# Sharing projection half products over eight attention head pairs, and reordering the last visit's scaling

## The chip, the cores and the metric

The kernel runs on one core of a Trainium2 chip. The metric is the device time of one execution in microseconds (us), taken as the median of several runs. A program of one core has five engines that run side by side and wait for each other by semaphores: PE (matrix products), DVE and ACT (element-wise work), POOL (element-wise work and some transfers) and SP (issues most transfers).

## The reference

One layer with two parallel branches, a Mamba-2 scan and a causal attention with forget gates, merged and projected. Only the attention and the products around it matter here:

```python
proj = h @ w_in            # -> z_ssm, xBC, dt, q, k, v, f, z_att, g_ssm, g_att
for blk in range(seqlen // 128):
    s = q[blk] @ k[:q1].T * scale + fcum[q] - fcum[k]     # causal
    outs.append(softmax(s) @ v[:q1])
y_att  = o * silu(z_att)
merged = sigmoid(g_ssm) * (y_ssm @ w_branch_ssm) + sigmoid(g_att) * (y_att @ w_branch_att)
out    = x + rmsnorm(merged @ w_out)
```

Sequence 1024, model width 1024, 16 heads of 64, all in float32. Products of two float32 matrices are formed from high and low parts (`h`, `l`), so each 512-column product over one 128-row block takes three matmuls.

## The kernel before, in words

Every projection is a Strassen-like scheme with seven products for two units of 128 columns: a `Pair` has steps 1 to 7, each one product of prepared weights (`wop`) with one prepared operand (`x0` to `x6`, here named by the tiles: x0 is b11, x1 b21, x2 -b22, x3 t1, x4 -t2, x5 t3, x6 t4). A step has 12 matmuls and is cut into two *halves* of six. A `Stream` holds all steps in one fixed list and hands them out half by half (`stream.halves(n)`), so that PE has work while another phase waits. With each half go the preparations: weights for the step three places on (lines L351, L352), the results (L404, L412, L414 to L418), the operands of the next weight matrix (L265 loads, L277 to L281 splits into high and low), and gate products (L1062).

The attention phase runs over eight head pairs (two heads each, `hp` 0 to 7) with six *visits* `g` 0 to 5, in all 48 visits `m`. A visit belongs to two query blocks against one half of the keys. It issues in this order: the scores (`scores`: matmuls into tiles `s`, then on DVE the running minimum L1467 and on ACT the exponential L1471 with row sums), the weighted values of the visit before (`weighted`: tiles `av`), some halves of the stream ("ahead"), the transposes of the probabilities into tiles `pt` and their copies `p` (L1508 on DVE, L1510 on ACT), and some more halves ("behind"). `s` and `pt` share four PSUM banks.

After every second visit the row sums of a group of rows are complete. Such a group `n` (0, 1 or 2 of a head pair) goes through a chain: `scale` makes the factors 1/l (L1375, L1376 for group 2; L1379 to L1384 for the others) in the tile `ns`, PE turns them (tile `pt` or, at the very end, `tp`), ACT copies them to `st` (L1393) and sends them to DRAM (L1394), `take` reads them back spread over all partitions as `rb` (SP, L1400), and one visit later `out` multiplies the attention outputs by them (L1431, L1432; L1425 for group 2). For the last head pair `out(1)` also forms the differences that the next weight matrix needs (L1556, L1557) and splits them into x4, x5 and x2 at once; it issues no transfer. The tiles `st`, `rb`, the gate loads and the results named `th` share one ring of four buffers.

`room(m)` decides how many halves visit `m` gets: the halves that are left up to step 6 of the first pair of `w_branch_att` (`ends[4]`), times the visit's share of the weights that are left. That step needs an operand that only the last rows of the attention make. A scheduler then orders the instructions of each engine; those that are pinned keep their program order.

The loop over the visits, with the two places that the change touches, begins at line 1640:

```python
            for hd, which in end(m - 2):
                if hd.last and which:
                    hd.out(which)
            ...
            ahead, behind = room(m)
            stream.halves(ahead)
            for hd, which in end(m):
                hd.scale(which)
```

`end(m)` gives the head pair and group that visit `m` completes.

Of the kernel before, what the change touches and what calls it, by code (L numbers as in the profile page):

```python
# [19 lines left out]
NK = D // P  # L20
# [66 lines left out]
def hybrid_layer(ctx: ExitStack, tc, a, out):  # L87
# [1047 lines left out]
    with tc.tile_pool(name="pro", bufs=1, reuse_waits="tile", side="right") as pro, tc.tile_pool(  # L1135
# [37 lines left out]
        def turned(tiles, k):  # L1173
            pt = prop.tile([P, HALF], F32, tag="pt", bufs=2, name="pt")
            for j in range(4):
                turn(pt[:, j * P : (j + 1) * P], tiles[j][:, k * P : (k + 1) * P]) 
            return pt
# [117 lines left out]
    with tc.tile_pool(name="att", bufs=1, reuse_waits="tile", side="right") as ap, tc.tile_pool(  # L1295
# [26 lines left out]
        def load_q(hp, pair):  # L1322

            t = ap.tile([P, 2, 256], F32R, tag="q", bufs=2, name="q")
            for n, dram in enumerate((qh_dram, ql_dram)):
                nc.sync.dma_start(t[:, n, :].bitcast(F32), dram[hp, :, pair[1] * P : pair[1] * P + 256])
            q[hp, pair] = t

        def load_k(hp, h):

            t = k[hp, h] = ap.tile([P, 2, HALF], F32R, tag=f"k{h}", name="k")
            for n, dram in enumerate((kh_dram, kl_dram)):
                nc.sync.dma_start(t[:, n, :].bitcast(F32), dram[hp, :, half(h)])
            f = fb[hp, h] = ap.tile([P, 2, HALF], F32, tag=f"fb{h}", name="fb")
            nc.sync.dma_start(f, f_dram[2 * hp : 2 * hp + 2, half(h)].unsqueeze(0).to_broadcast([P, 2, HALF]))

        def load_v(hp, h):
            v[hp, h] = ap.tile([P, 4, P], F32, tag=f"v{h}", name="v")
            pin(nc.sync.dma_start(v[hp, h], v_dram[hp][:, 4 * h : 4 * h + 4, :]))
# [96 lines left out]
        heads = {}  # L1436

        def scores(hp, g, u):

            pair, h = GROUPS[g]  # L1440
            i = pair[u]
            w = min(HALF, (i + 1) * P - h * HALF)
            s = [pp.tile([P, HALF], F32, tag="s", bufs=4, name="s") for e in range(2)]
            t, keys = q[hp, pair], k[hp, h]
            isl = slice(i % 2 * P, i % 2 * P + P)
            ops = [(t[:, x, isl], keys[:, y, 0:w]) for x, y in ((0, 0), (0, 1), (1, 0))]
            diagonal = h == i // 4
            for m, (x, y) in enumerate(ops):
                for e in range(2):
                    mm(  # L1450
                        s[e][:, 0:w], x[rows[e]], y[rows[e]], start=(m == 0), stop=(m == 2 and not diagonal),
                        skip_group_check=True,
                    )
            if diagonal:
                for n, (x, y) in enumerate(corner):
                    for e in range(2):
                        mm(
                            s[e][:, w - P : w], x[rows[e]], y[rows[e]], start=False, stop=(n == 1),
                            skip_group_check=True,
                        )  # L1460
            hd = heads[hp]
            for e in range(2):
                o = ex[:, e, u, 0:w]
                nm = hd.at(hd.nm, i, h, e)
                with tc.high_priority():
                    pin(
                        nc.vector.tensor_tensor_reduce(  # L1467
                            o, s[e][:, 0:w], fb[hp, h][:, e, 0:w], 1.0, 3.0e38, ALU.add, ALU.min, nm
                        )
                    )  # L1470
                    pin(nc.scalar.activation(o, o, AF.Exp, scale=-1.0, bias=nm, accum_out=hd.at(hd.sm, i, h, e)))  # L1471
# [42 lines left out]
        def weighted(hp, g, b, first, p, start, stop):  # L1514
            pair, h = GROUPS[g]
            n = (7 - pair[0]) // 2 if pair[0] > 3 else 2
            hd = heads[hp]
            if n not in hd.av:
                hd.av[n] = pp.tile([P, HALF], F32, tag="av", bufs=1, name="av")
            c0 = 256 * h if n < 2 else pair[1] * P  # L1520
            for e in range(2):
                mm(
                    hd.av[n][rows[e], c0 + first * P : c0 + 256], v[hp, h][:, b % 4, rows[e]], p[:, e, first:, :],
                    start=start, stop=stop, skip_group_check=True,
                )

        state, deferred = {}, []

        def fetched(name, j):
            y = small("y")  # L1530
            nc.sync.dma_start(y, ops_a.block(name, j))
            return y

        def difference_tile():
            return ap.tile([P, HALF], F32, tag="x", bufs=1, name="x")
# [44 lines left out]
        def loads(m):  # L1580

            hp, g = divmod(m, 6)
            more = hp + 1 < NK
            if g == 0:
                if hp:
                    load_v(hp, 0)
                if not m:

                    for j in range(KH):
                        stream.line += ops_s.differences(j, difference_tile, small)  # L1590
            if g == 1:
                load_q(hp, (3, 2))
            if g == 2 and more:
                load_k(hp + 1, 1)
            if g == 3:
                load_q(hp, (1, 0))
                if more:
                    load_v(hp + 1, 1)
                if hp >= KH:
                    state["t"] = difference_tile()  # L1600
                    nc.sync.dma_start(state["t"], ops_a.block("t1", hp - KH))
            if g == 4 and more:
                load_q(hp + 1, (7, 6))
            if g == (5 if more else 4) and hp >= KH:
                state["y"] = fetched("b11", hp - KH)
            if g == 5 and more:
                load_k(hp + 1, 0)
                load_q(hp + 1, (5, 4))

        def end(m):  # L1610

            hp, g = divmod(m, 6)
            if 0 <= hp < NK and g % 2:
                yield heads[hp], g // 2
# [7 lines left out]
        for _ in range(14):  # L1622
            stream.half()

        weights = (1.1, 1.1, 1.1, 1.1, 0.75, 0.95, 1.05, 0.85)

        rooms = [1.15, 1.15, 0.8, 1.15, 1.1, 0.75]
        left = [sum(rooms) * sum(weights)]

        def room(m):  # L1630

            share = weights[min(m // 6, NK - 1)] * rooms[m % 6]
            to = stream.steps.index((ends[4], 6))
            n = round((2 * (to - stream.at) - (stream.run is not None)) * share / left[0])
            left[0] -= share
            behind = n // 2 if n > 3 else min(max(n - 1, 0), 1)
            return n - behind, behind

        made = []
        for m in range(6 * NK + 1):  # L1640

            if m < 6 * NK:
                hp, g = divmod(m, 6)
                if not g:
                    heads[hp] = Heads(hp)
                for u in range(2):
                    scores(hp, g, u)
            for one in made:
                weighted(*one)
            for hd, which in end(m - 1):  # L1650
                hd.free(which)
            if m == 6 * NK:
                stream.release()
                heads[NK - 1].out(2)
                break
            for hd, which in end(m - 2):
                if hd.last and which:
                    hd.out(which)
            for fn in deferred:
                fn()  # L1660
            deferred.clear()
            stream.release()
            for hd, which in end(m):
                hd.settle(which)
            ahead, behind = room(m)
            stream.halves(ahead)

            for hd, which in end(m):
                hd.scale(which)
                hd.load_gates(which)  # L1670
            loads(m)
            made = turned(hp, g, list(end(m - 1)))
            for hd, which in end(m - 2):
                if not hd.last or not which:
                    hd.out(which)
            if m == 6 * NK - 1:
                tp = pp.tile([P, HALF], F32, tag="s", bufs=4, name="tp")
                heads[hp].turn(2, tp)
                heads[hp].send(2, tp)
            stream.hold()  # L1680
            stream.halves(behind)
            for hd, which in end(m if m == 6 * NK - 1 else m - 1):
                hd.take(which)
# [59 lines left out]
```

## Time and profile before

| what | value |
|---|---|
| median of 3 runs | 1290.88 us (1290.15 to 1292.31) |
| the profiled execution, its own time | 1291.84 us |
| its span (first to last instruction) | 1290.1 us |
| granted TensorE clock over the span | 0.996 |
| attention phase in the trace | about 687 to 1133 us |

The page of the profile gives busy times by engine, the chain of work that ended last, and groups of instructions by line. The trace answers queries: the waits of an engine in a stretch, busy times and granted clock in stretches, and the instructions in order of time, each with the idle time before it and what ended it in square brackets. A half product of the stream shows as six matmuls of 128x512 with the operand's name (`x0h`, `x0l`).

### The profile page before, as it was taken

To read this page: it belongs to the slowest core of one execution; us is meant where nothing else is said; L and a number is where in the kernel's file an instruction comes from. 1 tells how busy PE (TensorE), PEld (TensorE's weight loads), DVE (VectorE), ACT (ScalarE), POOL (GpSimd) and SP (SyncE) were. 2 spreads that over 40 slices of the span, in tenths; PEclk is the share of its full clock that TensorE was granted. 3 is DMA by queue.
4 is the path that set the end of the run, shared out by engine and by line. 5 is a ranking of instruction groups with operands and counts; after the bars stand their busy time and mean duration, and the time that the engine had idled before them with its cause. 6 is when DMAs were issued, how large, how long until landed. Compare 5 with 4: busy or idle time off the path is not lost.

```text
span 1290.1 us, 20992 instructions
## 1 busy us (share of the span) xinstructions
PE 1255.2 (97%) x7054; PEld 987.4 (77%) x7054; DVE 1005.1 (78%) x1994; ACT 795.6 (62%) x1738; POOL 258.8 (20%) x250
## 2 busy tenths in 40 slices
PE   5999999999999999999999999999999999899997
PEld 3688888787888888888877777777777776678886
DVE  7988886987788978997767567666798767776975
ACT  7745665556665665566556666666786567644754
POOL 4000440013300330124101121110001102146052
PEclk9999999999999999999999999999999999999999
DMA  8232552646336533653365666667787568556932
GB/s 297 72 113 76 154 154 90 190 150 182 131 110 201 186 126 105 217 168 119 132 204 202 200 222 204 206 215 224 259 261 249 199 212 268 191 188 195 360 111 101
DMA packets 153515, 233.57 MB, mean 181 GB/s; under 512 B 15968, under 2 KB 61504, under 8 KB 153408
## 3 DMA queue, kind: packets, MB, share of 16 engines
q1 hardware_dynamic: 137408, 197.14, 48.0%
q10 hardware_dynamic: 11136, 19.11, 3.9%
q0 software_dynamic: 4864, 15.99, 3.2%
q8 instruction: 55, 0.90, 0.3%
q14 instruction: 52, 0.43, 0.1%
HBM read 162.99 MB, written 72.34 MB: 182 GB/s over the span
## 4 chain that ended last, share of the span: by engine, by line
PE 76%; DVE 8%; DMA 7%; ACT 4%; issue 2%; SPq 1%; ACTq 0%; DVEq 0%
PE pb L130 32%; PE pc L130 19%; PE pd L130 6%; PE s L130 5%; PE pt L133 5%; PE av L130 4%; PE yps L130 2%; DVE wop L352 2%; DMA raw<-in_wu 1%; DMA xt<-in_x 1%; PE st L130 1%; DVE sum L357 1%; DMA st_dram<-st 1%; PE tr L133 1%; PE tr_v L133 1%
## 5 line engine op out<-in xcount | busy, mean ns | idle before, releaser
L351 ACT ACTIVATE wop<-sum 128x512 fp32r<-128x512 f32 x180 | 112.5, 626 | 111.4 <-DVE sum L357 52.3
L352 DVE TENSOR_TENSOR wop<-sum,wop 128x512 fp32r<-128x512 f32 x180 | 137.1, 763 | 55.0 <-ACT wop L351 54.0
L1471 ACT ACTIVATE ex<-ex,nm 128x512 f32<-128x512 f32 (+1 forms) x192 | 116.3, 607 | 65.8 <-DVE nm L1467 62.5
L404 ACT ACTIVATE s<-pb 128x512 f32<-128x512 f32 x144 | 85.2, 591 | 99.7 <-PE pb L130 97.7
L130 PE MATMUL pc<-x3h,wop 128*128 128x512 f32 x384 | 130.6, 397 | 1.6 <-DVE th L414 1.3
L130 PE MATMUL pc<-x2h,wop 128*128 128x512 f32 x384 | 130.7, 398 | 0.6 <-DVE u L416 0.6
L130 PE MATMUL pb<-x0h,wop 128*128 128x512 f32 x384 | 131.0, 399 | 0.0
L130 PE MATMUL pb<-x5h,wop 128*128 128x512 f32 x384 | 129.8, 396 | 1.1 <-ACT s L404 1.1
L130 PE MATMUL pb<-x6h,wop 128*128 128x512 f32 x384 | 129.4, 395 | 1.3 <-ACT s L404 1.3
L352 DVE TENSOR_TENSOR wop<-raw,wop 128x512 fp32r<-128x512 f32 x144 | 101.0, 703 | 36.3 <-ACT wop L351 35.9
L130 PE MATMUL pb<-x4h,wop 128*128 128x512 f32 x384 | 129.2, 395 | 0.0
L1467 DVE CUSTOM_DVE_ANT_0 ex<-s,fb 128x512 f32<-128x512 f32 (+1 forms) x192 | 97.2, 552 | 20.0 <-PE s L130 19.9
L351 ACT ACTIVATE wop<-raw 128x512 fp32r<-128x512 f32 x144 | 89.7, 623 | 21.1 <-PE pc L130 13.6
L130 PE MATMUL pd<-x1h,wop 128*128 128x512 f32 x288 | 96.3, 394 | 0.0
L130 PEld LDWEIGHTS pc<-x3h,wop 128*128 128x128 f32 x384 | 72.3, 188 | 18.9 <-DVE th L414 1.7
L130 PEld LDWEIGHTS pb<-x5h,wop 128*128 128x128 f32 x384 | 72.1, 188 | 18.7 <-ACT s L404 2.2
L130 PEld LDWEIGHTS pc<-x2h,wop 128*128 128x128 f32 x384 | 72.1, 188 | 18.4 <-issue 2.8
L130 PEld LDWEIGHTS pb<-x6h,wop 128*128 128x128 f32 x384 | 72.1, 188 | 18.2 <-issue 1.9
L130 PEld LDWEIGHTS pb<-x0h,wop 128*128 128x128 f32 x384 | 72.7, 189 | 17.3 <-issue 2.7
L130 PEld LDWEIGHTS pb<-x4h,wop 128*128 128x128 f32 x384 | 72.3, 188 | 17.1 <-issue 2.3
L133 PE MATMUL pt<-ident,ex 128*128 128x128 f32 x576 | 75.4, 274 | 1.6 <-DVE nm L1467 0.6
L130 PE MATMUL s<-k,q 64*128 64x512 f32 (+3 forms) x576 | 73.6, 368 | 2.0 <-ACT p L1510 1.5
(310 smaller groups left out, 2915.8 us busy)
## 6 DMA issues: line engine op xcount, KB each, us to landing
raw<-in_wu SPq DMA_DIRECT2D x128, 256.0 KB
csb<-cs_dram SPq DMA_DIRECT2D x32, 256.0 KB
fb<-f_dram SPq DMA_DIRECT2D x16, 512.0 KB
rb<-st_dram SPq DMA_DIRECT2D x48, 128.0 KB
wd<-in_wo SPq DMA_DIRECT2D x40, 128.0 KB
xt<-in_x SPq DMA_DIRECT2D x8, 512.0 KB
gs_dram<-th ACTq DMA_DIRECT2D x16, 256.0 KB
qh_dram<-th ACTq DMA_DIRECT2D x16, 256.0 KB
```

What stands on the lines that cost most here:

```text
L130: return tc.keep_in_program_order(nc.tensor.matmul(*args, **kw))
L133: return tc.keep_in_program_order(nc.tensor.transpose(out_, in_, idn))
L351: nc.scalar.activation(op[:, 0], src, AF.Copy)
L352: nc.vector.tensor_tensor(op[:, 1], src, op[:, 0], ALU.subtract)
L357: self.adds.tensor_tensor(t, x, y, ALU.add)
L404: nc.scalar.activation(s, ps, AF.Copy)
L1467: nc.vector.tensor_tensor_reduce(o, s[e][:, 0:w], fb[hp, h][:, e, 0:w], 1.0, 3.0e38, ALU.add, ALU.min, nm)
L1471: pin(nc.scalar.activation(o, o, AF.Exp, scale=-1.0, bias=nm, accum_out=hd.at(hd.sm, i, h, e)))
```

## The change

It has two parts. The first is the table that shares out the halves. There are 156 of them from the start of the attention phase up to step 6 of `ends[4]` in both versions. Worked through `room`, the eight head pairs get 22, 22, 22, 22, 16, 16, 20 and 16 halves before, and 18, 18, 18, 19, 21, 19, 21 and 22 after. Inside a pair before, visits of the first four pairs have 4, 4, 3, 4, 4 and 3 halves, where 4 is two ahead and two behind and 3 is two ahead and one behind; in pairs 4, 5 and 7 it is 3, 3, 2, 3, 3 and 2, where 2 is one ahead and one behind. After, every visit of the first three pairs has 3, and no visit has 2. The last visit of all (pair 7, `g` 5) has one ahead and one behind before, and two ahead and two behind after.

The second part moves `out(1)` of the last head pair in that last visit from ahead of the halves to behind `scale(2)`, so that the last factors 1/l stand ahead of the products of the rows before them.

```diff
-        weights = (1.1, 1.1, 1.1, 1.1, 0.75, 0.95, 1.05, 0.85)
-        rooms = [1.15, 1.15, 0.8, 1.15, 1.1, 0.75]
-        left = [sum(rooms) * sum(weights)]
+        weights = (1.0, 1.0, 1.0, 1.0, 1.02, 1.02, 1.05, 1.15)
+        rooms = [1.1, 1.1, 0.85, 1.1, 1.05, 0.85]
+        left = [sum(rooms) * sum(weights) - weights[-1] * rooms[-1] + 1.4]

         def room(m):
-            share = weights[min(m // 6, NK - 1)] * rooms[m % 6]
+            share = weights[m // 6] * rooms[m % 6] if m < 6 * NK - 1 else 1.4
             to = stream.steps.index((ends[4], 6))
             n = round((2 * (to - stream.at) - (stream.run is not None)) * share / left[0])
             left[0] -= share
+            if m == 6 * NK - 1:
+                return n // 2, n - n // 2
             behind = n // 2 if n > 3 else min(max(n - 1, 0), 1)
             return n - behind, behind
...
             for hd, which in end(m - 2):
-                if hd.last and which:
+                if hd.last and which and m < 6 * NK - 1:
                     hd.out(which)
...
             for hd, which in end(m):
                 hd.scale(which)
                 hd.load_gates(which)
+            if m == 6 * NK - 1:
+                heads[hp].out(1)
+                for fn in deferred:
+                    fn()
+                deferred.clear()
```

The number of instructions on each engine stays the same. The places where the order differs most for what follows are in the last visit.

PE in the last visit, before: after the weighted values of visit 46 one half (x3, step 5 of `ends[4]`), six transposes of probabilities, and the turn of the last factors (`tp<-ident,ns`).

```order
L130 MATMUL av<-p,v 64x128 x2
L130 MATMUL pc<-x3h,wop 128x512
L130 MATMUL pc<-x3l,wop 128x512
L130 MATMUL pc<-x3h,wop 128x512 x2
L130 MATMUL pc<-x3l,wop 128x512
L130 MATMUL pc<-x3h,wop 128x512
L133 MATMUL pt<-ident,ex 128x128 x6
L133 MATMUL tp<-ident,ns 8x128
L130 MATMUL pc<-x3h,wop 128x512
```

The same place after: two halves (x6, step 4 of the last pair of `w_branch_ssm`) stand ahead of the transposes.

```order
L130 MATMUL av<-p,v 64x128 x2
L130 MATMUL pb<-x6h,wop 128x512
L130 MATMUL pb<-x6l,wop 128x512
L130 MATMUL pb<-x6h,wop 128x512 x2
L130 MATMUL pb<-x6l,wop 128x512
L130 MATMUL pb<-x6h,wop 128x512 x2
L130 MATMUL pb<-x6l,wop 128x512
L130 MATMUL pb<-x6h,wop 128x512 x2
L130 MATMUL pb<-x6l,wop 128x512
L130 MATMUL pb<-x6h,wop 128x512
L133 MATMUL pt<-ident,ex 128x128 x6
L133 MATMUL tp<-ident,ns 8x128
```

Step 5 with x3, which surrounded the turn before, now stands wholly behind it.

DVE in the last visit, before: after the last running minimum (`nm`) come the products of `out(1)` with `rb`, and the factors (L1375, L1376) between them.

```order
L1467 ISA nm 128x1
L1431 TENSOR_TENSOR o<-o,rb 128x512
L1432 TENSOR_TENSOR zr<-o 128x256
L1375 RECIPROCAL sm<-sm 128x8
L1556 TENSOR_TENSOR x<-zr,x 128x512
L1376 TENSOR_SCALAR ns<-sm 128x8
L1557 TENSOR_TENSOR y<-x,y 128x512
```

The same place after:

```order
L1467 ISA nm 128x1
L281 TENSOR_TENSOR x3l<-x3l,x3h 128x512
L1375 RECIPROCAL sm<-sm 128x8
L1376 TENSOR_SCALAR ns<-sm 128x8
L1431 TENSOR_TENSOR o<-o,rb 128x512
L281 TENSOR_TENSOR x3l<-x3l,x3h 128x512
L1432 TENSOR_TENSOR zr<-o 128x256
L281 TENSOR_TENSOR x3l<-x3l,x3h 128x512
L1556 TENSOR_TENSOR x<-zr,x 128x512
```

The factors are now ahead of L1431, and the low parts of two of the four blocks of x3 are behind it; by their addresses these are blocks 0 and 1, which step 5 takes first.

ACT in the last visit after, with the semaphores that each instruction waits for:

```order
L1471 ACTIVATE ex,sm<-ex,nm 128x128 [waits DVE_49] x2
L280 ACTIVATE x3h<-x3l 128x512 [waits DMAHW7_49]
L280 ACTIVATE x3h<-x3l 128x512 [waits DMAHW0_49]
L412 ACTIVATE th<-pb 128x512 [waits DMAHW5_49,DMAHW0_49,DMAHW7_49,DVE_49,PE_49]
L351 ACTIVATE wop<-raw 128x512 [waits DMAHW4_49]
L277 ACTIVATE x2h<-x2l 128x512 [waits DMAHW6_49]
L277 ACTIVATE x2h<-x2l 128x512 [waits DMAHW1_49]
L1510 ACTIVATE p<-pt 128x512 [waits PE_49]
L1510 ACTIVATE p<-pt 128x2x128 [waits Activation_49]
L1393 ACTIVATE st<-tp 8x128 [waits DMASW1_49,DMASW0_49,PE_49]
```

The result copy L412 takes over the buffer of `rb`, so its wait for DVE is a wait for L1431; the last two `p` copies and the copy of the turned factors `st` stand behind it. Before, L412 stood ahead of the last exponentials:

```order
L412 ACTIVATE th<-pb 128x512 [waits DMAHW1_49]
L1471 ACTIVATE ex,sm<-ex,nm 128x256 [waits DVE_49] x2
L1471 ACTIVATE ex,sm<-ex,nm 128x128 [waits DVE_49] x2
L1510 ACTIVATE p<-pt 128x512 [waits PE_49]
L1510 ACTIVATE p<-pt 128x2x128 [waits Activation_49]
L277 ACTIVATE x4h<-x 128x512 [waits DVE_49]
L1393 ACTIVATE st<-tp 8x128 [waits DMAHW6_49,DMASW0_49,PE_49]
```

There the `p` copies followed the exponentials directly. One visit earlier, in visit 46, the copy of group 1's factors (`st<-pt`, L1393) names a DVE semaphore among its waits before (by its value, L1062, the gate product whose buffer it takes); after, it names two transfers and PE alone.

## The prediction

> **What bounds the kernel now.** I read the page first, for which engine the end hangs on, from its busy times and its chain:
>
> ```profile
> PE 1255.2 (97%) x7054; PEld 987.4 (77%) x7054; DVE 1005.1 (78%) x1994; ACT 795.6 (62%) x1738; POOL 258.8 (20%) x250
> PE 76%; DVE 8%; DMA 7%; ACT 4%; issue 2%; SPq 1%; ACTq 0%; DVEq 0%
> ```
>
> PE is busy 97% of the span. The change leaves PE's matmuls as they are, so it can only win back time in which PE stands still or runs slowly, or add such time. Next I read the busy times by head pair (stretches between the last factors of successive pairs; the columns are the stretch and its length, then PE, PEld, DVE, ACT, POOL, granted clock, DMA share, GB/s):
>
> ```profile
> 738.80:798.00 59.20, 59.20 (x400) 45.25 (x399) 39.22 (x106) 36.79 (x92) 9.22 (x11) 1.00 0.65 208
> 915.00:965.00 50.00, 49.36 (x348) 36.74 (x347) 44.71 (x117) 41.91 (x104) 2.16 (x4) 1.00 0.83 274
> 965.00:1015.00 50.00, 50.00 (x364) 37.89 (x362) 39.52 (x110) 31.65 (x85) 4.86 (x9) 1.00 0.69 226
> 1068.80:1129.20 60.40, 54.40 (x359) 38.91 (x357) 46.04 (x115) 41.72 (x104) 11.08 (x14) 0.97 0.72 233
> ```
>
> Pair 1, with 22 halves, has no idle PE. Pair 5, with 16, has none either, so 16 halves were enough there. Pair 4 loses 0.64 us with DVE at 89%. Pair 7, with 16, loses 6.0 us (part of them before and after the pair's own visits) and its clock is below 1. So the time lies in the last pair. The waits of PE from 1090 to 1140 us, and for comparison from 870 to 980 us (total, count, longest):
>
> ```profile
> PE tp L133 <- DVE ns L1376: 3.3, 1, 3.3
> PE s L130 <- ACT p L1510: 1.2, 2, 1.1
> PE pb L130 <- ACT s L404: 0.7, 1, 0.7
> PE pt L133 <- ACT ex L1471: 0.6, 1, 0.6
> PE pt L133 <- DVE nm L1467: 0.3, 1, 0.3
> ```
>
> ```profile
> PE s L130 <- DVE p L1508: 0.4, 2, 0.2
> PE s L130 <- ACT p L1510: 0.3, 1, 0.3
> ```
>
> The longest wait is for the factors of the last group. The chain in order of time shows why they are late:
>
> ```profile
> 1117.93 0.10 ACT st L1393
> ...
> 1118.25 3.71 DMA st_dram<-st
> ...
> 1121.98 0.61 ACT th L412
> ...
> 1122.61 0.69 DVE th L1062
> ...
> 1123.84 3.46 DMA rb<-st_dram
> ...
> 1127.40 0.70 DVE o L1431
> ...
> 1129.20 0.18 DVE ns L1376
> ...
> 1129.42 0.27 PE tp L133
> ```
>
> The factors (L1376) stand on DVE behind L1431 of the preceding rows, and L1431 waits for `rb`, which has gone through DRAM and through the ring of four buffers (L412 and L1062 must free one first). The factors themselves need none of this.
>
> Each of the two longer waits is followed by a slow PE. The stretches:
>
> ```profile
> 1107.41:1118.52 11.11, 10.02 (x71) 7.60 (x70) 9.86 (x23) 8.16 (x21) 1.63 (x2) 1.00 0.41 127
> 1118.52:1123.84 5.32, 5.07 (x37) 3.22 (x37) 4.26 (x9) 3.69 (x8) 0.42 (x2) 0.68 0.63 193
> 1126.15:1129.42 3.27, 0.00 (x1) 0.00 (x1) 1.99 (x6) 0.98 (x3) 0.00 (x0) 1.00 0.07 23
> 1129.42:1132.97 3.55, 3.55 (x15) 1.97 (x15) 2.55 (x4) 2.92 (x6) 0.00 (x0) 0.64 0.01 5
> 1132.97:1139.90 6.93, 6.24 (x26) 4.87 (x25) 5.62 (x9) 3.20 (x6) 1.79 (x2) 0.94 0.85 267
> ```
>
> A clock of 0.68 over 5.32 us costs 5.32 x 0.32 = 1.70 us; 0.64 over 3.55 and 0.94 over 6.93 cost 1.28 + 0.42 = 1.70 us. So each fall costs 1.70 us.
>
> **The change, part by part.**
>
> *Factors ahead of `out(1)`.* Two short DVE instructions move ahead of L1431, L1432, L1556, L1557 and the splits of `out(1)`. The 3.27 us wait of the turn goes, since the factors then need only the last row sums, and the two halves ahead (one more than before) cover those. What is late next is `out(1)` itself, and what stands behind it: on DVE the low parts of x3 blocks 0 and 1, on ACT the result copy L412, the last two `p` copies and `st`. PE wants x3 first. These rows give PE's path from the turn of group 1's factors to it:
>
> ```profile
> 1089.74 0.62 PE L130 MATMUL s<-k,q 64*128 64x256 f32 x6
> 1092.76 0.50 PE L130 MATMUL pc<-x3h,wop 128*128 128x512 f32 x1
> 1100.25 0.50 PE L130 MATMUL pb<-x0h,wop 128*128 128x512 f32 x1
> 1103.10 0.78 PE L133 MATMUL pt<-ident,ex 128*128 128x128 f32 x3
> 1115.12 0.27 PE L133 MATMUL pt<-ident,ns 128*8 128x128 f32 x1
> 1115.80 0.48 PE L130 MATMUL pb<-x6h,wop 128*128 128x512 f32 x1
> 1118.52 1.09 PE L130 MATMUL s<-k,q 64*128 64x256 f32 x6 [1.09 <-ACT p L1510]
> 1125.33 0.82 PE L133 MATMUL pt<-ident,ex 128*128 128x128 f32 x6
> ```
>
> From the turn to the half behind 0.68; that half 1118.52 - 1.09 - 1115.80 = 1.63; scores and values of a visit of this shape 1092.76 - 1089.74 = 3.02; two halves 1103.10 - 1100.25 = 2.85; six transposes and a turn about 0.8. PE begins x3 about 9.0 us after the turn and needs its low part at 9.3. The other path is `st`, DRAM, `rb`, L1431 and one split. It took 1127.40 - 1117.93 = 9.47 us from `st` to L1431, of which 1123.84 - 1121.96 = 1.9 were the ring, leaving 7.6; a later trip took less:
>
> ```profile
> 1117.93 0.27 ACT L1393 ACTIVATE st<-pt 8x128 f32<-8x128 f32 x1 [0.69 <-PE pb L130]
> ...
> 1129.85 0.25 ACT L1393 ACTIVATE st<-tp 8x128 f32<-8x128 f32 x1
> ...
> 1135.17 0.69 DVE L1425 TENSOR_TENSOR zr<-o,rb 128x512 f32<-128x512 f32 x1 [0.19 <-DMA rb<-st_dram]
> ```
>
> The second trip is 1135.17 - 1129.85 = 5.3 us. With 1.3 for L1431 and a split, 6.6 to 8.9 us from `st`. `st` came 2.8 us after the turn. Of that 0.69 was idle, for the buffer that L1062 held, a wait it no longer has; the rest, 2.1, was other work of ACT, and the order now has one operation of some 0.5 less there (six after the exponentials instead of seven). So I let it start between 0.3 (at once) and 1.6 us after the turn. So x3 is ready 6.9 to 10.5 us after the turn, against 9.3: from 2.4 early to 1.2 late. I take 0.3, nearer to early since the ring's wait is gone. If `st` starts at 2.8 again, it is 11.7, 2.4 late, and with a fall of the clock 4.1. `out(1)` feeds x4 only one half pair later, and step 6 waits for nothing else of it.
>
> *Four halves in the last visit, three everywhere early.* The first four pairs lose halves behind the transposes: their visits with two behind fall to one. That cover serves the `p` copies, which free the banks for the next scores. Before, 29 visits had one behind, and together they show 0.7 + 1.25 us of such waits, 0.067 each. After, 36 have one, 7 more: 0.5 us; bounds 0 and 7 x 1.09 = 7.6. No visit has one half ahead any more (seven did), so the 0.61 us wait of transposes for exponentials goes. Of the 1.09 + 0.16 us in visit 47, most came from `st` 2.8 us late, since the `p` copies stand behind it on ACT: it goes with that wait.
>
> *More halves in pairs 4 to 7.* Pair 7 gets 22 instead of 16 and so the operand splits of x0 to x6 within fewer visits. Pair 4 shows what that costs where DVE is at 89%: 0.64 us in 50. I take 0.8 us for pair 7; bounds 0 and, for pairs 4 and 7 each, twice that, 3.2.
>
> *Sum.* Gone: 3.27 + 1.25 + 0.61 = 5.1 idle, and two falls of the clock, 3.4: 8.5 us. Come: 0.3 + 0.5 + 0.8 = 1.6. Net 6.9. The 0.69 us wait for L404 stays, and the rest of the program behind it is in the same PE order. Against the profiled execution's own 1291.84 us that is 1284.9. The median of the runs shown is 0.96 lower, at 1290.88, which would give 1284.0. I forecast midway: **1284.5 us**.
>
> [...] The second fall followed a wait of 3.27 us, the first one of 1.09 us. Elsewhere a wait as long left the clock alone:
>
> ```profile
> 675.66 0.50 PE L130 MATMUL pc<-x3h,wop 128*128 128x512 f32 x1 [1.28 <-DVE th L414]
> ```
>
> ```profile
> 675.66:679.00 3.34, 3.33 (x15) 2.76 (x16) 2.81 (x5) 1.71 (x4) 0.00 (x0) 1.00 1.05 402
> ```
>
> So 1.09 us of idleness alone does not make a fall; what stood around it differs (16 transposes and small score matmuls here, dense halves there). [...]
>
> **The rivals.**
>
> *The first fall stays* (transposes and small products cause it, not the gap): the gain is 1.70 us less, 1286.2. For it, the row at 675 us; against it, the many other visits of the same shape with a clock of 1.00 and no gap.
>
> *A new wait in the old one's place:* `st` is late again, L1431 holds x3 and the `p` copies, PE stands 2.4 us and the clock falls: 4.1 instead of 0.3, so 1288.3. For it, DVE and ACT both stand behind one trip through DRAM now; against it, the ring's waits are gone and PE has 1.4 us more to do first.
>
> *Slower: the early visits lose their cover.* In pairs 0 to 3, 15 visits go from two halves behind to one. If ACT (62% there) or DVE's own `p` copies are late, scores wait for banks. At the 1.09 us of visit 47 each it costs 15 x 1.09 = 16.4 us, 15.9 more than I took: 1300.4. It turns the result beyond 0.2% slower from (6.9 + 2.6) / 15 = 0.63 us a visit. Against it, pair 1's row: two of its six visits already have one half behind and PE is never idle; and pair 5 with one behind in all six.
>
> *No net change:* the waits move into pairs 4 to 7, where both DVE and transfers are densest (pair 4: DMA 0.83), and eat the gain: 1290.9.
>
> **How the numbers follow.** Forecast 0.55, first fall stays 0.15, new wait 0.12, early visits 0.10, no net change 0.08. A measurement of this kernel can tell about 0.2%, 2.6 us, from no change: faster means below 1288.3, slower above 1293.5. The first two and half of the third are faster, 0.76; the other half and nearly all of the last are the same, 0.13; the early visits and a rest of the last slower, 0.11. The range: below, everything gone and nothing come, 1290.88 - 8.5 = 1282.4; above, the new wait with the density term at its bound of 3.2 instead of 0.8, 1288.3 + 2.4 = 1290.7. That holds the first three, 0.82.
>
> **What would show it.** In the changed profile: no wait of `tp` for L1376; a clock of 1.00 from 1090 to 1140 us, or one fall (first rival); waits of scores for `p` below 2 us in all over the phase; `st` of visit 46 within 1.6 us of its turn; x3's first matmul behind `tp` without a wait above 1 us. The forecast is wrong if PE's idle time from 687 to 1137 us and the falls of the clock together do not come down from about 10 (the waits quoted, 6.8, and 3.4) to about 3 us.

## The result, and the profile after

After takes 1286.72 us (median of 10 runs, 1282.37 to 1289.42), before 1290.65 us beside it (10 runs, 1287.28 to 1294.19): a ratio of 0.9965, 95% interval 0.9953 to 0.9977. That is faster, inside the range, and 2.2 us above the forecast of 1284.5. Runs of one kernel differ by up to 10 us, so everything below goes by ratios, and a profile is one sample. The profiled execution of after took 1288.76 us.

First the page of after, its busy times:

```profile
PE 1253.9 (97%) x7054; PEld 987.4 (77%) x7054; DVE 1010.0 (78%) x1994; ACT 794.7 (62%) x1738; POOL 259.8 (20%) x250
```

PE is 1.3 us less busy than before and DVE 4.9 us more, which says nothing of where the time moved. The busy times by stretch do, from the first scores of the phase to the wait for L404 at its end, cut at 1090 us; before, then after:

```profile
686.77:1090.00 403.23, 402.10 (x2772) 305.41 (x2773) 288.77 (x780) 269.78 (x678) 51.41 (x70) 1.00 0.68 221
1090.00:1137.05 47.05, 40.64 (x253) 28.18 (x251) 37.45 (x86) 30.28 (x76) 8.01 (x10) 0.93 0.60 194
```

```profile
686.19:1090.00 403.81, 397.62 (x2735) 300.59 (x2735) 286.33 (x771) 264.84 (x668) 49.81 (x68) 0.99 0.65 216
1090.00:1134.61 44.61, 43.77 (x288) 32.55 (x287) 38.39 (x93) 34.60 (x86) 10.19 (x11) 1.00 0.69 234
```

Behind 1090 us PE's idle time goes from 6.41 to 0.84 us and the clock from 0.93 to 1.00 (47.05 x 0.07 = 3.3 us): some 8.9 us won. Ahead of 1090 us the idle time goes from 1.13 to 6.19 us and the clock to 0.99. So the last pair gained what was forecast, and most of it was given back earlier. PE's waits in after from 687 to 1145 us (total, count, longest):

```profile
PE pt L133 <- ACT ex L1471: 2.5, 2, 2.2
PE pt L133 <- DVE nm L1467: 2.5, 4, 1.5
PE s L130 <- ACT p L1510: 0.8, 2, 0.6
PE pb L130 <- ACT s L404: 0.7, 1, 0.7
PE s L130 <- DVE p L1508: 0.3, 1, 0.3
```

They add up to 6.8 us, as in before, but the two of the last pair (`tp` for L1376, scores for `p`) are gone but for 0.15 us, and two kinds that were 0.6 us each are 2.5 us each.

**The last visit of after**, from the timelines of PE, ACT and DVE:

```profile
1117.64 0.27 PE L133 MATMUL pt<-ident,ns 128*8 128x128 f32 x1
1119.21 0.25 ACT L1393 ACTIVATE st<-pt 8x128 f32<-8x128 f32 x1
...
1125.32 1.14 ACT L280 ACTIVATE x3h<-x3l 128x512 fp32r<-128x512 f32 x2
1126.57 0.60 ACT L412 ACTIVATE th<-pb 128x512 f32<-128x512 f32 x1
...
1125.68 0.17 DVE L1376 TENSOR_SCALAR ns<-sm 128x8 f32<-128x8 f32 x1
1125.76 0.69 DVE L1431 TENSOR_TENSOR o<-o,rb 128x512 f32<-128x512 f32 x1
...
1126.37 0.81 PE L133 MATMUL pt<-ident,ex 128*128 128x128 f32 x6
1127.03 0.27 PE L133 MATMUL tp<-ident,ns 128*8 128x128 f32 x1
1127.06 0.48 PE L130 MATMUL pc<-x3h,wop 128*128 128x512 f32 x1
```

The factors (L1376) come ahead of L1431, the turn `tp` stands directly behind the transposes, and x3 directly behind `tp`: no row has an idle time.

**Pair 5 of after.** The last factors (L1376) of pair 4 stand at 947.98 us, so what follows is the first visit of pair 5; the expectations further down call this place pair 4. Timeline of ACT, then of PE; then the busy times of the stretch in which the transposes wait and of the one behind it:

```profile
956.57 0.33 ACTq L622 DMA_DIRECT2D ga_dram<-th  x1
956.94 1.16 ACT L280 ACTIVATE x1h<-x1l 128x512 fp32r<-128x512 f32 x2 [4.47 <-DMA fb<-f_dram]
...
960.89 0.69 PE L133 MATMUL pt<-ident,ex 128*128 128x128 f32 x2 [2.25 <-ACT ex L1471]
962.19 1.81 PE L133 MATMUL pt<-ident,ex 128*128 128x128 f32 x6 [0.61 <-DVE nm L1467]
...
958.64:960.89 2.25, 0.01 (x2) 0.00 (x1) 2.25 (x7) 2.25 (x6) 0.54 (x1) 0.95 0.89 287
960.89:967.50 6.61, 6.00 (x21) 4.67 (x21) 5.92 (x13) 5.98 (x16) 1.08 (x2) 0.50 0.96 354
```

ACT stood for 4.47 us at the store of a gate (L622), which ACT issues itself. The store waited for the broadcast load into `fb`, which has nothing to do with its data; in the trace the two only count on the same DMA semaphore (number 102), one after the other. x1's splits, the maxima (L1467) and the exponentials (L1471) came that much later. PE stood 2.25 and 0.61 us. The clock fell at the end of the first wait (0.95 over it) and was 0.50 over the 6.61 us behind it, which is 3.3 us more, 0.3 of them while PE stood anyway.

**Pair 7 of after**, its second visit, DVE and PE:

```profile
1082.74 0.69 DVE L1062 SCALAR_TENSOR_TENSOR th<-th 128x512 f32<-128x512 f32 x1 [5.68 <-DMA th<-gs_dram]
...
1087.13 0.33 PE L133 MATMUL pt<-ident,ex 128*128 128x128 f32 x1 [1.46 <-DVE nm L1467]
```

The same kind of standing: DVE waits for a load of the gate, with the maxima queued behind L1062.

### The profile page after: what moved, and what is told of

Read it like the earlier page. It is cut to its first block, busy times and chain, and to the rows that moved or that the text cites. A ratio compares the mean times of both kernels' runs of the same rounds, so it can differ in the third digit from the quotient of the medians.

```text
span 1287.0 us, 20996 instructions
## 1 busy us (share of the span) xinstructions
PE 1253.9 (97%) x7054; PEld 987.4 (77%) x7054; DVE 1010.0 (78%) x1994; ACT 794.7 (62%) x1738; POOL 259.8 (20%) x250
## 4 chain that ended last, share of the span: by engine, by line
PE 73%; DVE 9%; DMA 8%; ACT 5%; issue 3%; SPq 1%; POOL 0%; ACTq 0%; DVEq 0%; POOLq 0%
PE pb L130 30%; PE pc L130 17%; PE pd L130 6%; PE av L130 5%; PE s L130 5%; PE pt L133 5%; PE yps L130 2%; DVE wop L352 2%; DMA raw<-in_wu 1%; DVE sum L357 1%; DMA xt<-in_x 1%; PE st L130 1%; DVE xs L771 1%; PE tr L133 1%; ACT wop L351 1%
## 5 line engine op out<-in xcount | busy, mean ns | idle before, releaser
L1471 ACT ACTIVATE ex<-ex,nm 128x512 f32<-128x512 f32 (+1 forms) x192 | 116.2, 606 | 71.8 <-DVE nm L1467 67.7
L404 ACT ACTIVATE s<-pb 128x512 f32<-128x512 f32 x144 | 85.1, 591 | 98.3 <-PE pb L130 95.3
L1467 DVE CUSTOM_DVE_ANT_0 ex<-s,fb 128x512 f32<-128x512 f32 (+1 forms) x192 | 96.9, 552 | 17.9 <-PE s L130 17.9
L133 PEld LDWEIGHTS pt<-ident,ex 128*128 128x128 f32 x576 | 67.4, 142 | 15.1 <-DVE nm L1467 4.3
```

The costliest lines, as they stand in the source:

```text
L133: return tc.keep_in_program_order(nc.tensor.transpose(out_, in_, idn))
L404: nc.scalar.activation(s, ps, AF.Copy)
L1467: nc.vector.tensor_tensor_reduce(o, s[e][:, 0:w], fb[hp, h][:, e, 0:w], 1.0, 3.0e38, ALU.add, ALU.min, nm)
```

## The experiments

The theory was that the gain is the last visit's and that the evenly shared table gives part of it back where engines that work in order stand behind late transfers. The rivals: order or halves alone make the gain; ACT and DVE are simply full at this place; what it shows is one run's accident.

### One half of the change at a time

Before with the order alone:

```
             for hd, which in end(m - 2):
-                if hd.last and which:
+                if hd.last and which and m < 6 * NK - 1:
                     hd.out(which)
...
+            if m == 6 * NK - 1:
+                heads[hp].out(1)
+                for fn in deferred:
+                    fn()
+                deferred.clear()
             loads(m)
```

> Before's table of halves (one ahead and one behind in the last visit), with only out(1) of the last pair moved behind the factors of the last group. Theory 1 (the gain lies in the last visit; order and halves each carry a part): the 3.27 us wait of the turn for the factors goes and with it the fall of the clock behind it, 1.7 us, but PE now has one half less on its way to x3, so x3 waits up to 2.9 us for its low part, and the 1.09 us wait with its fall further ahead may stay: 1286 to 1289 us where before has 1290.7. Theory 2 (the order alone does all of it): as after or below, 1283 to 1286.7. Theory 3 (only the halves count; without them the wait for the factors just turns into one for x3, as long and with the same fall): 1290 to 1291.

1287.79 us, ratio 0.9975 (0.9963 to 0.9987): inside the range of theory 1. The wait of `tp` is gone, but PE waits elsewhere in the last pair (timeline of PE), and behind the first of these waits the clock falls once (0.85 and 0.81 in the two stretches of 5 us from 1100 us):

```profile
1102.15 0.33 PE L133 MATMUL pt<-ident,ex 128*128 128x128 f32 x1 [0.88 <-DVE nm L1467]
...
1130.59 0.50 PE L130 MATMUL pb<-x4l,wop 128*128 128x512 f32 x1 [1.32 <-DVE x4l L278]
```

The x3 that it was to wait for came in time; x4 did not, with one half less in between. Theory 2 is not ruled out: 1287.79 lies above its range, but the interval holds after's 0.9965, and the quotients of the medians are 0.9968 here (before took 1291.86 us beside it) and 0.9970 for after.

After with the table alone (the diff above taken out of after):

> After's table of halves (four in the last visit), with out(1) at its old place ahead of the factors. Theory 1: two more halves give PE about 2.8 us more work there; the one ahead covers 1.4 of the 3.27 us wait, so some 1.9 us of it stay, with a fall of the clock or without: 1288.5 to 1290.5. Theory 2 (the order does all of it): the table brings nothing by itself, and its denser late pairs cost: 1291 to 1294. Theory 3 (only the halves count): as after, 1286.7.

1293.10 us, ratio 1.0019 (1.0006 to 1.0033). The time is the one of theory 2, but the reason is another than its denser pairs alone. PE, DVE and ACT in the last visit of that kernel:

```profile
1122.08 0.27 PE L133 MATMUL tp<-ident,ns 128*8 128x128 f32 x1
1126.80 0.50 PE L130 MATMUL pc<-x3h,wop 128*128 128x512 f32 x1 [4.45 <-ACT x3h L280]
...
1120.28 0.69 DVE L1431 TENSOR_TENSOR o<-o,rb 128x512 f32<-128x512 f32 x1
1121.34 0.16 DVE L1376 TENSOR_SCALAR ns<-sm 128x8 f32<-128x8 f32 x1
...
1126.13 1.13 ACT L280 ACTIVATE x3h<-x3l 128x512 fp32r<-128x512 f32 x2
```

`tp` does not wait here either, though L1431 still stands ahead of the factors: with more halves in the pair, `rb` lands in time. But `out(1)` now also puts its operand copies ahead of x3's on ACT (x3h at 1126.13; in after at 1125.32, ahead of L412), and PE stands 4.45 us for them. So the table needs the order: alone it costs 0.19%, both together win 0.35%, and these intervals are far apart. That the order needs the table is not shown: alone it wins 0.25%, which cannot be told from both.

### Is it the even table?

After with before's weights and rooms, the last visit kept at four:

```
-        weights = (1.0, 1.0, 1.0, 1.0, 1.02, 1.02, 1.05, 1.15)
+        weights = (1.1, 1.1, 1.1, 1.1, 0.75, 0.95, 1.05, 0.85)
-        rooms = [1.1, 1.1, 0.85, 1.1, 1.05, 0.85]
+        rooms = [1.15, 1.15, 0.8, 1.15, 1.1, 0.75]
```

> After's order and four halves in the last visit, with before's weights and rooms for all other visits: per pair 22, 22, 22, 21, 15, 16, 20, 18 halves where after has 18, 18, 18, 19, 21, 19, 21, 22. Theory 1 (the evenly shared table gives back some 4 us in pairs 4 to 7, where more halves put transfers and operand copies into fewer microseconds): no wait for exponentials and no fall of the clock in pair 4, 1281.5 to 1284. Rival (the table costs nothing; what after shows in pairs 4 and 7 varies from run to run and would come here as well): 1286.7 as after. Rival (one half ahead in visits 2 and 4 of pairs 4 and 7 leaves transposes waiting for exponentials): 1287 or more with waits on the exponentials of over 2 us in all.

1290.31 us, ratio 0.9992 (0.9979 to 1.0006): theory 1 missed. Without the even table the kernel is slower than after, and the intervals lie apart, if barely. The last rival has the time but not its waits. They are for ACT's `p`, 4.8 us in all, and the largest has the same cause as in after, at another place (chain in order of time, then PE and the stretch):

```profile
930.82 3.82 DMA rb<-st_dram
...
934.72 0.33 ACTq L622
...
935.09 1.09 ACT p L1510 x2
```

```profile
935.74 0.32 PE L130 MATMUL s<-k,q 64*128 64x128 f32 x1 [1.91 <-ACT p L1510]
...
935.00:940.00 5.00, 4.09 (x26) 2.64 (x26) 4.08 (x16) 4.24 (x13) 0.54 (x1) 0.66 0.97 317
```

A gate store holds ACT until an `rb` load has landed, 2.2 us. With either table a store meets a late load; the table decides which. Before's profile has one as well: behind a gate store at 953 us ACT stands 2.3 us for a load of `q`, and PE waits no more than 0.3 us there.

### The gate stores off ACT's queue

After with L622 on GpSimd's queue:

```
-            nc.scalar.dma_start(dram[i, :, half(ch)], t[ch])
+            pin(nc.gpsimd.dma_start(dram[i, :, half(ch)], t[ch]))
```

> After, with the stores of the tanh gates (L622) issued on GpSimd's queue instead of ScalarE's. In after's profile such a store held ScalarE 4.47 us in pair 4, until an unrelated broadcast load into fb had landed; exponentials came late, PE stood 2.25 and 0.61 us and its clock was 0.50 for 6.6 us. Theory 1 (this standing still is what the density of pair 4 costs): no such waits and no fall in pair 4, 2.9 + 3.3 = 6.2 us less if every run of after has it, 1.5 to 6 us less than after in the median, 1281 to 1285. Rival (ScalarE and VectorE are simply full in pair 4): the exponentials are as late without the store, 1286.7 as after. Rival (GpSimd's stores hold up its own additions or stores, which feed PE): 1287 to 1290.

1284.95 us, ratio 0.9953 (0.9936 to 0.9969), at the upper end of theory 1's range. Beside later kernels it was run once more:

> The kernel of e4_gate_store once more (after, with the gate stores on GpSimd's queue), because six runs gave 0.9953 with an interval that still touches after's 0.9965. Theory (ScalarE standing behind gate stores costs after 1 to 3 us): 0.993 to 0.9955, no wait for exponentials above 0.6 us in pair 4. Rival (no more than chance): 0.996 to 0.997.

1284.72 us, 0.9951 (0.9933 to 0.9968). And after itself once more:

> After itself once more, as a reference for the runs beside it and for a second profile of the same program. Theory (where PE stands is set by the program; the microseconds vary with when transfers land): waits on exponentials or their maxima in pair 4 and pair 7 again, the falls of the clock in other places or numbers, ratio to before 0.9965 +- 0.0015. Rival (pair 4's wait was one run's accident): no wait above 0.5 us in pair 4.

1286.83 us, 0.9965 (0.9951 to 0.9978). Each of the two intervals of the stores moved overlaps after's, but both runs lie on the same side of after by nearly the same. The repeated after has the waits of pair 5 again, behind the same store, and half the slow time (timeline of PE, then a stretch, then ACT's wait):

```profile
957.57 0.44 PE L133 MATMUL pt<-ident,ex 128*128 128x128 f32 x2 [1.38 <-ACT ex L1471]
958.87 1.25 PE L133 MATMUL pt<-ident,ex 128*128 128x128 f32 x6 [0.86 <-DVE nm L1467]
...
960.00:965.00 5.00, 5.00 (x25) 4.01 (x24) 4.38 (x8) 5.00 (x13) 1.08 (x2) 0.66 1.04 389
...
ACT x1h L280 <- DMA fb<-f_dram: 3.6, 1, 3.6
```

The run of the table alone shows the same wait of ACT, with 2.6 us. So it is no accident of one run.

Pairs 4 and 5 in one stretch, 900 to 1010 us, of before, after, after again, the stores moved, and the stores moved again, in this order:

```profile
900.00:1010.00 110.00, 109.36 (x767) 82.70 (x765) 89.68 (x234) 81.61 (x205) 7.02 (x13) 1.00 0.76 247
```

```profile
900.00:1010.00 110.00, 106.08 (x707) 79.62 (x706) 83.77 (x221) 78.15 (x193) 7.22 (x12) 0.97 0.71 237
```

```profile
900.00:1010.00 110.00, 106.85 (x716) 80.07 (x713) 85.13 (x224) 78.22 (x191) 7.36 (x13) 0.98 0.73 244
```

```profile
900.00:1010.00 110.00, 107.31 (x736) 80.14 (x735) 86.40 (x227) 77.64 (x191) 12.29 (x22) 1.00 0.74 251
```

```profile
900.00:1010.00 110.00, 106.73 (x722) 80.15 (x720) 84.94 (x225) 78.50 (x193) 11.53 (x20) 1.00 0.73 246
```

Idle time is 0.64 us in before, 3.92 and 3.15 in after, still 2.69 and 3.27 with the stores moved. What the move takes away is the falls of the clock: the wait for exponentials shrinks to 0.5 us, and waits for `p` (0.9 and 1.4 us) come further on. Over all runs the mean granted clock is 0.9972 and 0.9971 in after (18 runs), 0.9987 and 0.9987 with the stores moved (12 runs): 0.0015 of 1285 us is 1.9 us, about all of the difference between the medians (1.8 and 2.1). Just ahead of these waits ACT stood 4.47 us in after, and DVE, which needs ACT's split, 3.60 us, so they were not full there, and that rival falls for what the move takes away.

The wait for `p` that is left with the stores moved has a late load behind it, too, in the second of these runs: DVE stood 1.92 us at L1557 for the load of `y`, with the `p` copy (L1508) behind it in its order. DVE there:

```profile
961.52 0.69 DVE L1557 TENSOR_TENSOR y<-x,y 128x512 f32<-128x512 f32 x1 [1.92 <-DMA y<-ya_dram]
```

The same move on three other kernels. Before's weights with after's order and four halves:

> Before's weights and rooms, after's order and four halves in the last visit, with the gate stores on GpSimd's queue. In the kernel with these weights alone, a gate store held ScalarE in pair 4 until an rb load had landed; PE stood 1.91 us there and its clock fell. Theory (the stores on ScalarE's queue make this loss, wherever the table puts them): no wait above 0.5 us in pair 4, 1.91 + 1.7 us less, ratio 0.9963 to 0.998 against 0.9992. Rival (one half ahead in these visits is too little for ScalarE): the wait stays, 0.9992.

1288.86 us, 0.9967 (0.9956 to 0.9979), against 0.9992 without it: the theory's time, and the 1.91 us wait is gone. The size is uncertain: the intervals touch, and the quotients of the medians are 0.9981 and 0.9988. But a wait of 1.69 us for DVE's `p` with a fall came at 941 us, so "no wait above 0.5" missed.

Before:

> Before, with only the gate stores moved to GpSimd's queue. Before's profile shows no wait of PE above 0.3 us in pairs 0 to 5, so there is nothing for the move to win: ratio 0.999 to 1.001 (theory: the move helps only where the table has put a gate store behind a late load). Rival (the stores cost ScalarE time everywhere): ratio 0.997 or below. Rival (GpSimd's own work is held up): above 1.001.

1289.57 us, 0.9989 (0.9975 to 1.0003). This cannot be told from no change.

Before's table with after's order:

> Before's table of halves, with both other changes: out(1) of the last pair behind the last factors, and the gate stores on GpSimd's queue. The order alone gave a ratio of 0.9975 and its profile shows no gate store that holds up ScalarE in pairs 4 and 5. Theory (the stores cost only where the table puts them behind a late load, and the even table adds its four halves in the last visit): 0.997 to 0.998, 3 to 4 us above the even table with the same two changes (0.994 to 0.995). Rival (with the stores out of the way the even table brings nothing): 0.994 to 0.9955.

1286.72 us, 0.9971 (0.9959 to 0.9983), against 0.9975 without the move: the theory's ratio, with a smaller distance to the even table than it named. The even table is worth 0.10% with the stores on ACT (0.9975 to 0.9965; the intervals overlap) and 0.19% with them moved (0.9971 to 0.9952; they overlap here, too).

### The gate loads of pair 7

The stores moved, and L1062 a half step later (`stream.after(2, ...)` for `stream.after(1, ...)`):

> After with the gate stores on GpSimd's queue, and L1062 (the product with the gate loaded from gs_dram) issued two half steps after its block instead of one, so that VectorE does not come to it before its load has landed. Theory (VectorE's standing at L1062, 7.6 us in after from 1000 to 1140 us against 1.1 in before, is what makes maxima and exponentials late in pair 7): its wait falls below 2 us, the 0.99 + 0.28 us of PE in pair 7 go, and a fall with them where it comes: 0.5 to 3 us below the kernel with the stores alone, ratio 0.992 to 0.995. Rival (pair 7's waits come from VectorE's or ScalarE's own work): the waits of PE stay, ratio 0.9953. Rival (the later product holds its buffer of the ring a half longer, and loads and stores of the ring come late): ratio 0.997 or more.

1283.79 us, 0.9939 (0.9924 to 0.9954), the fastest kernel here, though not apart from the two runs of the stores alone. The mechanism did not work: the waits of DVE for this load are 6.7 us, and PE's in pair 7 0.93 and 0.28. So its margin over them is not shown to come from the edit.

The load moved to GpSimd's queue instead (L1053, beside the stores):

> After with the gate stores on GpSimd's queue, and also the loads th<-gs_dram (L1053) on that queue instead of SyncE's. In after such a load stands on SyncE's queue behind an x0l load, which waits some 9 us for PE, and VectorE then waits 5.1 to 5.7 us for it at L1062 in pair 7 with the maxima behind. Theory (this is where pair 7's 1.45 us of PE comes from): VectorE's wait for the load below 2 us, PE's waits in pair 7 below 0.5 us, 1 to 2.5 us below the stores alone, ratio 0.9925 to 0.9945. Rival (GpSimd issues the load as late, behind its ms_dram stores): the waits stay, 0.994 to 0.9955. Rival (GpSimd's queue of transfers is slower to land): 0.996 or more.

1289.47 us, 0.9996 (0.9981 to 1.0011). At the place in pair 7 PE now waits 0.28 and 0.26 us, as the theory had it; DVE's wait did not fall below 2 us. The loads are late five times instead of two, and one of them meets the last visit (waits of DVE; PE; the stretches behind it):

```profile
DVE th L1062 <- DMA th<-gs_dram: 8.2, 5, 3.2
```

```profile
1121.44 1.74 PE L133 MATMUL pt<-ident,ex 128*128 128x128 f32 x6 [2.01 <-ACT ex L1471]
...
1120.00:1125.00 5.00, 3.11 (x10) 1.64 (x11) 3.80 (x15) 4.21 (x13) 1.08 (x2) 0.77 0.76 262
1125.00:1130.00 5.00, 5.00 (x19) 3.42 (x17) 3.24 (x6) 2.70 (x8) 0.54 (x1) 0.55 0.17 66
```

1.15 + 2.25 = 3.4 us of clock, and 2.01 of idle time: the gain is taken back and more.

### Fewer halves in the late pairs

The stores moved, and the weights (1.08, 1.08, 1.08, 1.08, 0.9, 1.0, 1.03, 1.0):

> After with the gate stores on GpSimd's queue and other weights, (1.08, 1.08, 1.08, 1.08, 0.9, 1.0, 1.03, 1.0): per pair 21, 21, 21, 21, 16, 18, 18, 20 halves where after has 18, 18, 18, 19, 21, 19, 21, 22; the last visit has 2 and 3. Theory 1 (fewer halves in pair 4 spread its transfers, and nothing else is lost): PE's waits in pairs 4 to 7 below 1.5 us in all, ratio 0.992 to 0.994. Rival (the number of halves in pair 4 does not matter once the stores are gone; waits just stand elsewhere): 0.994 to 0.9955. Rival (visits with one half ahead lose more than the others win, as with before's weights): 0.9965 or more.

1293.66 us, 1.0022 (1.0010 to 1.0034): slower than before. The theory falls; the last rival has the side. The edit is no test of fewer halves where after's waits stood: that is pair 5, which goes from 19 halves to 18. Pair 4, with 16, now has waits of its own, the longest for `p` (timeline of PE, and one past the phase):

```profile
958.02 1.10 PE L130 MATMUL s<-k,q 64*128 64x256 f32 x6 [1.48 <-DVE p L1508]
...
1146.87 0.50 PE L130 MATMUL pb<-x6l,wop 128*128 128x512 f32 x1 [1.59 <-DVE x6l L281]
```

Why it loses as much as 0.7% against the even table is open: its profile shows 7.2 us of waits in the phase and one fall, not clearly worse than after's 6.8 and two. Of the 3.0 us by which its span is longer than after's, 2.4 lie behind the phase, 1.59 of them at the wait shown.

## Why the prediction was right or wrong

**Factors ahead of `out(1)`: the effect right, half of the reason wrong.** The 3.27 us are gone. `st` started 1119.21 - 1117.64 = 1.57 us after its turn, at the edge of the 0.3 to 1.6 allowed, L1431 came 6.55 us after it (5.3 to 7.6), and x3 waited for nothing: 0 where 0.3 was taken. But the run of the table alone shows `tp` without a wait in the old order as well. There the price of the old order is x3 standing 4.45 us behind `out(1)`'s copies on ACT, which the prediction did not have in its list for the old order.

**The falls of the clock: right for the last pair.** 3.4 us were counted as gone, and the clock is 1.00 from 1090 to 1134 us. The first fall did not stay when its wait went, so the rival built on its staying falls. That no fall would come anywhere else was taken without a reason; it belongs to the term below.

**Four halves in the last visit, fewer early: right.** The 1.25 + 0.61 us went, but for a last 0.15 us of scores waiting for `p`. Of the rival of the slower early visits nothing is seen: from 687 to 890 us the only wait above 0.2 us is 0.27 us at 692.49. Waits of scores for `p` are 0.8 + 0.3 us over the phase, below the 2 allowed.

**More halves in pairs 4 to 7: the term that was mis-sized.** 0.8 us were taken, with a bound of 3.2. Measured: from 900 to 1010 us 3.92 - 0.64 = 3.3 us more idle time and 3.3 us of clock, and 1.4 us more in pair 7 (1.46 + 0.28 against 0.34): 8.0 us in the profiled run, with the 0.3 us of slow clock that fell into a wait counted twice. In the repeat it is 2.5 + 1.70 + 1.4 = 5.6. The step that failed is the choice of the row: the price was scaled from DVE's share of 89%. By the runs with the stores moved, the price hangs on which late transfer an engine meets in its own queue (4.47 us of ACT at the gate store in after, 1.92 us of DVE at the load of `y` with the stores moved once more), and on the clock, which the sum did not let fall anew. The rival "no net change" named the place, pairs 4 to 7 and their transfers, and that is where the miss lies.

**The sum.** 8.5 us gone and 5.6 to 8.0 come makes 0.5 to 2.9, where 6.9 was forecast and the medians differ by 3.9. The phase itself, from the first scores to the wait for L404, went from 450.28 us to 448.42 in the profiled run; the span is 3.1 us shorter, and the rest, 0.6 us ahead of the phase and 0.7 behind it, is none of the prediction's terms. Some 1.3 us in the phase these waits and falls do not account for, and it stays open where they are. The prediction's own test, idle time and falls from about 10 to about 3 us, was not met: 6.8 + 3.3 = 10.1 in the profiled run, 5.6 + 1.7 = 7.3 in the repeat. By that test the sum failed. The time fell into the range because the range left room for a density of 3.2 and a new wait; the wait came elsewhere. That the median came within 2.2 us of the forecast is in part luck.

## What to carry to other kernels

When work is moved from one stage to another, look in the new stage not only at busy shares but at every DMA that a computing engine issues itself or waits for in order: a store on ACT's queue can hold exponentials behind a load that it has nothing to do with (4.47 us in after). Of two edits of one place one can lose alone and do no harm beside the other, so undo them one at a time. And price a stall on PE with its fall of the clock, as an uncertain extra: a fall cost 1.70 us in before and 3.4 us in after, and some gaps had none behind them.

## What the runs showed of the hardware

**The clock was low for 3.41 us or for twice that, and a gap's length alone did not decide it.** In before the clock is 0.50 from 1120.15 to 1123.56 us and again from 1130.39 to 1133.80 us, 3.41 us each time, and 1.00 between. In after it is 0.50 from 960.66 to 967.49 us, 6.83 us; this began within its wait of 2.25 us. A stretch of 0.66 over 5 us (two profiles above) is a loss of 1.70 us, as much as 3.4 us at 0.50. Falls followed 1.38 + 0.86 us (after again), 1.91 us (before's weights) and as little as 0.88 us (the order alone). None followed 1.88 us in the last pair of the kernel with before's weights, nor 1.51 us in the kernel with the later product:

```profile
1120.85 1.09 PE L130 MATMUL s<-k,q 64*128 64x256 f32 x6 [1.88 <-ACT p L1510]
...
1120.00:1125.00 5.00, 3.90 (x38) 2.81 (x39) 4.97 (x11) 4.65 (x12) 2.22 (x2) 1.00 0.38 129
```

```profile
962.53 1.66 PE L130 MATMUL s<-k,q 64*128 64x512 f32 x12 [1.51 <-DVE p L1508]
...
960.00:965.00 5.00, 3.49 (x25) 2.20 (x25) 4.41 (x8) 2.81 (x7) 1.60 (x3) 1.00 0.97 354
```

**A store's wait was paid by the engine that issues it.** ACT, which issues the gate store, stood 4.47 us at it in after, 3.6 us in after again and 2.6 us with the table alone, each time until the load into `fb` had landed. With the store on GpSimd's queue ACT has no wait for that load in the phase.
